# Top-k threshold search in a two-layer kernel: a third row counted on ScalarE, the test for equals moved to VectorE, GpSimd's sums beside the search cut into four pieces

## The chip, the cores and the metric

The kernel runs on one core of a Trainium2 chip. The metric is the device time of one execution in microseconds (us); the time of a kernel is the median of its runs.

## The reference

Two layers on 1024 tokens (T) of width 1024, in fp32. The change is in the first one, `hybrid_layer`, whose mixing half projects the normalised input once (`h @ w_in`) and gives part of the columns to a sparse attention and the rest to an RWKV7 scan:

```python
def dsa_attention(...):
    score = jnp.einsum('bth,bths->bts', wi, relu(jnp.einsum('bthd,bsd->bhts'...)))
    score = jnp.where(causal[None], score, -jnp.inf)
    _, sel = lax.top_k(score, 256)          # the 256 best keys of each query
    ...                                     # attention over the selected keys only
def rwkv7_group(p, mu_shift, w0, w_decay_up, a0, w_aaa_up, w_gate_up, ...):
    p = p + mu_shift * (p_prev - p)         # p_prev: the token before
    r, k, v, wd, ad, gd = jnp.split(p, splits, axis=-1)
    w_log = -softplus(-(w0 + tanh(wd) @ w_decay_up)) - 0.5
    a = sigmoid(a0 + ad @ w_aaa_up)
    g = sigmoid(gd) @ w_gate_up
    ...                                     # the scan, a group norm, times g
```

The output projection, an FFN and a second block (convolution, chunked attention, FFN, a gated per-layer embedding) follow; the change leaves them alone.

## The kernel before, in words

The framework's tile scheduler fixes the order of every engine's instructions when the kernel is built, from its own model of durations; on the chip each engine (PE = TensorE, DVE = VectorE, ACT = ScalarE, POOL = GpSimd, SP = SyncE, which issues loads and stores) works through its list in order and waits on semaphores where a tile that it reads or overwrites is not ready. Changing the cost or the number of a few instructions may therefore change the order of others, far from them.

Every fp32 product is made of three matmuls on a high and a low part (`mm3`, L105 to L107). A weight block of 128 columns is loaded (`load_cols`), its high part copied by ScalarE (L88) and its low part computed by GpSimd (L89), both in `split_w`, and `fm` then issues 48 matmuls of 512 columns.

The stage of the change is opened at L1875 and holds two streams that share no data.

The **projections of RWKV** (`Rwkv.proj`, TensorE). Fourteen blocks of `w_in`; each result in PSUM (three buffers of 128x1024) goes through `shift`: ScalarE writes it scaled (L1019) and a second time scaled and moved by one token (L1021), GpSimd adds the two (L1022), SP stores it. After every three blocks come the small products of one quarter of the decay, a and gate columns (`wl`, `gl`): weights split by L1064 and L1065, two evictions with a sigmoid (L1072) and one of the gate (L1080). There are four such quarters, so four gate evictions.

The **threshold search** (`Dsa.topk`, VectorE). Query blocks 2 to 7 give six rows j = 0 to 5 of 128 queries by 128 * (j + 3) scores. The 256th largest score of each query is found bit by bit: 15 rounds on the upper 16 bits, one count, 16 rounds on the lower 16 bits, 32 rounds in all. A round counts the scores at or above a candidate in each row: rows j < A on ScalarE, by Sign with an accumulator (L855, after `nv`, L850), the rest on VectorE (L846). Then VectorE compares the counts with K (L865), updates f (L866) and makes the next candidate (L863). No round starts before the counts of the one before are in, from both engines.

After the search each of the six rows is made into a mask: L909 marks and counts the scores above the threshold, L911 says how many of the equal ones are needed, L912 (GpSimd) marks the equal ones, L913 numbers them, L914 and L915 combine, and ScalarE writes the mask (L916). The buffers of this stage then become those of the next, attention (`attend`, its first product is L940) beside the chunked scan of RWKV, whose loads SP issues (L1111 to L1115, kHL at L962, qT at L963).

Of the kernel before, what the change touches and what calls it, by code (L numbers as in the profile page):

```python
# [8 lines left out]
FP = mybir.dt.float32  # L9
# [6 lines left out]
ALU = mybir.AluOpType  # L16
AX = mybir.AxisListType
PSUM = bass.MemoryType.PSUM
T = 1024
# [5 lines left out]
class Core:  # L25
# [56 lines left out]
        self.nc.sync.dma_start(raw, w[k * 128:(k + 1) * 128, :])  # L82
        return raw

    def split_w(self, raw):
        shp = list(raw.shape)
        hl = self.wp.tile([shp[0], 2] + shp[1:], FR, name="whl", tag="whl", bufs=self.nhl)
        self.nc.scalar.activation(hl[:, 0], raw, AF.Copy)  # L88
        self.nc.gpsimd.tensor_sub(hl[:, 1], raw, hl[:, 0].bitcast(FP))  # L89
        return hl  # L90

    def after(self):
# [102 lines left out]
def fm(c, w, kt, act, m0=0, m=128):  # L195

    return fms(c, [w], kt, act, m0, m)[0]


def fms(c, ws, kt, act, m0=0, m=128):  # L200

    act = Feat(act) if isinstance(act, list) else act
    ps = [c.psum([m, T]) for _ in ws]
    for hf in range(2):
        sl = slice(hf * 512, hf * 512 + 512)
        for p, w in zip(ps, ws):
            c.mm3(p[:, sl], [((w[:, 0, k, m0:m0 + m], w[:, 1, k, m0:m0 + m]), (act.cols(k, 0, hf), act.cols(k, 1, hf))) for k in range(kt)])
    return ps
# [433 lines left out]
class Dsa:  # L642
# [187 lines left out]
    def topk(self, ap):  # L830

        c, nc = self.c, self.nc
        N, A = 6, 2
        st, sti, tk1 = self.tk
        cnt, K, sg, vs, gtc, need, pos, k1, f, cand, nv = (st[:, j] for j in range(11))
        pre, low = sti[:, 0], sti[:, 1]
# [43 lines left out]
        for j in range(N):  # L880
            x = self.sc[j + 2]
# [12 lines left out]
        for j in range(N):  # L894
            if j < A:
                nc.vector.tensor_scalar(K[:, j:j + 1], K[:, j:j + 1], -128.0 * (j + 3), None, op0=ALU.add)
            nc.vector.scalar_tensor_tensor(h[j].bitcast(U16), h[j], f[:, j:j + 1], self.sc[j + 2].bitcast(U16)[:, 0::2],
                                           op0=ALU.is_equal, op1=ALU.mult)
# [5 lines left out]
        for j in range(N):  # L904
            n = (j + 3) * 128
            x = self.sc[j + 2]
            gt = ap.tile([128, n], BF, name="gt", tag="junk", bufs=1)
            eq = ap.tile([128, n], BF, name="eq", bufs=2)
            nc.vector.scalar_tensor_tensor(gt, x, sg[:, j:j + 1], vs[:, j:j + 1].to_broadcast([128, n]), op0=ALU.mult, op1=ALU.is_gt,  # L909
                                           accum_out=gtc[:, j:j + 1])  # L910
            nc.vector.tensor_scalar(need[:, j:j + 1], gtc[:, j:j + 1], -1.0, 256.0, op0=ALU.mult, op1=ALU.add)  # L911
            nc.gpsimd.tensor_scalar(eq, x, pre.bitcast(FP)[:, j:j + 1], None, op0=ALU.is_equal)  # L912
            nc.vector.tensor_tensor_scan(x, one.to_broadcast([128, n]), eq, 0.0, op0=ALU.mult, op1=ALU.add)  # L913
            nc.vector.scalar_tensor_tensor(x, x, need[:, j:j + 1], eq, op0=ALU.is_le, op1=ALU.mult)  # L914
            nc.vector.scalar_tensor_tensor(x, x, -1.0, gt, op0=ALU.add, op1=ALU.add)  # L915
            nc.scalar.activation(self.mk[j + 2], x, AF.Copy, scale=-NEG)  # L916
# [63 lines left out]
class Rwkv:  # L980
# [35 lines left out]
    def shift(self, ap, ps, j, out, m=128):  # L1016

        nc = self.nc
        nc.scalar.activation(out, ps, AF.Copy, scale=self.mu1[:m, j:j + 1])  # L1019
        t = ap.tile([m, T], FP, name="sh", tag="xo", bufs=4)  # L1020
        nc.scalar.activation(t[:, 1:], ps[:, :T - 1], AF.Copy, scale=self.mu[:m, j:j + 1])  # L1021
        nc.gpsimd.tensor_add(out[:, 1:], out[:, 1:], t[:, 1:])  # L1022

    def proj(self, hT, gd32, ap, beside):
        c, nc, p = self.c, self.nc, self.p
        w = p["w_in"]
        t4 = lambda n: ap.tile([128, T], FP, name=n, tag="xo", bufs=4)
        lo = lambda n, m=128: ap.tile([m, 2, T], FR, name=n, tag="lo", bufs=2)
        cols = lambda j: fm(c, c.split_w(c.load_cols(w, 456 + j * 128, 128, 8)), 8, hT)

        def rkv(pr):
            for q in range(3):
# [6 lines left out]
        x = t4("xl")  # L1039
# [4 lines left out]
        x = t4("xl")  # L1044
# [4 lines left out]
        x = t4("xl")  # L1049
# [5 lines left out]
        for pr in range(4):  # L1055
            m = slice(pr * 128, pr * 128 + 128)
            raw = ap.tile([128, 3, 128], FP, name="wl_raw", bufs=1)
# [8 lines left out]
            for rows, b, dst in ((slice(0, 64), self.w0, self.sgd), (slice(64, 128), self.a0, self.ad)):  # L1066
                ps = c.psum([128, T])
                for hf in range(2):
                    s = slice(hf * 512, hf * 512 + 512)
                    c.mm3(ps[:, s], [((wt[rows, 0, 0], wt[rows, 1, 0]), (wl[rows, 0, s], wl[rows, 1, s]))])  # L1070
                x = t4("xo")
# [3 lines left out]
            for hf in range(2):  # L1075
                s = slice(hf * 512, hf * 512 + 512)
                c.mm3(ps[:, s], [((wt[:, 0, 1], wt[:, 1, 1]), (gl[:, 0, s], gl[:, 1, s])),
                                 ((wt[0:32, 0, 2], wt[0:32, 1, 2]), (gl2[:, 0, s], gl2[:, 1, s]))])
            x = t4("xo")
# [1033 lines left out]
```

## Time and profile before

| | us |
|---|---|
| median of three runs | 3777.41 (3772.05 to 3777.46) |
| the profiled execution | 3769.52 |
| its span in the profile | 3767.8 |
| TensorE / VectorE / ScalarE / GpSimd busy in the span | 3326.7 / 1980.7 / 1298.1 / 1127.8 |
| the stage of the change, first projection column to last mask | 276.6 to 550.6 |
| attention beside the scan, the next stage | 566 to 1164 |

The span is the time from the first to the last instruction of the profiled execution; its own time has 1.7 us around that. TensorE is busy 88% of the span, the other engines much less, but these are averages over stages with different limits: the stage of the change is 7% of the span, and what limits it is read from its own rows. [...]

### The profile page before, as it was taken

The page shows a single profiled execution, that of the slowest core. Times are in us where ns is not written, and L with a number is a line of the kernel's source. Part 1 is how long each engine was busy: PE and PEld are TensorE (multiplying, and loading weights), DVE is VectorE, ACT ScalarE, POOL GpSimd, SP SyncE. Part 2 cuts the span into 40 slices and gives each one's busy share as a digit, 9 for nine tenths or more (in the row PEclk, how much of TensorE's full clock was granted, in tenths as well). Part 3 has the DMA queues.
Part 4 walks back from the last instruction along what each step waited for, and adds up shares of the span by engine and source line. Part 5 has one row for each costly group of instructions (what it writes and reads, how often), then busy time and mean ns, then how long its engine had stood idle before and what let it go on. Part 6 is the DMA issues. An engine that isn't in the chain of part 4 may idle for free. (4 is left out here: it accounts for less than half of the span.)

```text
span 3767.8 us, 42121 instructions
## 1 busy us (share of the span) xinstructions
PE 3326.7 (88%) x16048; PEld 2689.4 (71%) x16048; DVE 1980.7 (53%) x3181; ACT 1298.1 (34%) x2177; POOL 1127.8 (30%) x1007
## 2 busy tenths in 40 slices
PE   3788767898996899999998999989978899998988
PEld 2666545676774688888887788778856788876767
DVE  5569987667643412221225210026733688879983
ACT  3354433333333321111113211246633444444332
POOL 3214245434325322222223222131143222223441
PEclk7888865566567999999999999999989999998989
DMA  4552232212124321111113122210043322213244
GB/s 168 154 165 90 75 108 89 76 35 71 31 72 144 118 60 47 51 45 51 51 45 112 53 70 84 102 56 10 19 141 127 95 84 82 81 56 140 93 149 149
DMA packets 252218, 324.67 MB, mean 86 GB/s; under 512 B 16383, under 2 KB 193504, under 8 KB 250992
## 3 DMA queue, kind: packets, MB, share of 16 engines
q1 hardware_dynamic: 250960, 321.75, 26.9%
q8 instruction: 126, 2.06, 0.2%
q14 instruction: 76, 0.62, 0.1%
q0 software_dynamic: 1056, 0.23, 0.0%
HBM read 241.63 MB, written 80.29 MB: 85 GB/s over the span
## 5 line engine op out<-in xcount | busy, mean ns | idle before, releaser
L89 POOL TENSOR_TENSOR whl<-wraw,whl 128x1024 fp32r<-128x1024 f32 (+1 forms) x128 | 286.6, 2244 | 882.5 <-ACT whl L88 879.2
L105 PE MATMUL ps<-h,whl 128*128 128x512 f32 x1216 | 477.8, 395 | 17.7 <-ACT h L214 13.6
L106 PE MATMUL ps<-h,whl 128*128 128x512 f32 x1216 | 478.5, 394 | 3.5 <-POOL h L215 3.5
L107 PE MATMUL ps<-h,whl 128*128 128x512 f32 x1216 | 477.1, 392 | 0.0
L105 PEld LDWEIGHTS ps<-h,whl 128*128 128x128 f32 x1216 | 230.9, 190 | 69.3 <-ACT h L214 15.9
L88 ACT ACTIVATE whl<-wraw 128x1024 fp32r<-128x1024 f32 (+1 forms) x128 | 125.2, 988 | 440.8 <-issue 225.0
L106 PEld LDWEIGHTS ps<-h,whl 128*128 128x128 f32 x1216 | 231.1, 190 | 54.4 <-POOL h L215 6.4
L107 PEld LDWEIGHTS ps<-h,whl 128*128 128x128 f32 x1216 | 231.0, 190 | 48.4
L532 DVE TENSOR_TENSOR silu<-silu,ps 128x1024 f32<-128x1024 f32 x22 | 26.9, 1221 | 431.8 <-PE ps L107 431.8
L288 PE MATMUL ps<-h,op 128*128 128x512 f32 x616 | 237.4, 391 | 6.1 <-ACT op L311 5.2
L289 PE MATMUL ps<-h,op 128*128 128x512 f32 x616 | 240.4, 390 | 0.0
L290 PE MATMUL ps<-h,op 128*128 128x512 f32 x616 | 239.9, 390 | 0.0
L597 PE MATMUL o<-pT,v 128*128 128x256 f32 (+1 forms) x640 | 156.7, 364 | 13.7 <-ACT pT L592 7.7
L313 POOL TENSOR_TENSOR op<-t,op 128x512 fp32r<-128x512 f32 x44 | 73.3, 1666 | 305.1 <-ACT op L311 268.9
L592 ACT ACTIVATE pT<-tp 128x512 fp32r<-128x512 f32 (+2 forms) x221 | 94.6, 444 | 186.7 <-PE tp L589 149.9
L1388 DVE SCALAR_TENSOR_TENSOR cv<-up,v_fw,cv 128x1023 f32<-128x1023 f32 x88 | 134.1, 1524 | 30.0 <-ACT cv L1386 29.8
L105 PE MATMUL ps<-wo,h 128*128 128x512 f32 x320 | 128.9, 412 | 18.9 <-ACT wo L1398 16.5
L288 PE MATMUL ps<-op,op 128*128 128x512 f32 x308 | 123.9, 405 | 24.1 <-ACT op L412 14.9
L106 PE MATMUL ps<-wo,h 128*128 128x512 f32 x320 | 129.8, 411 | 15.1 <-POOL wo L1399 15.1
L597 PEld LDWEIGHTS o<-pT,v 128*128 128x128 f32 x640 | 116.8, 238 | 36.4 <-ACT pT L592 14.0
L846 DVE TENSOR_SCALAR_CACHE_REDUCE junk<-h,tk 128x640 bf16<-128x640 int16 (+7 forms) x128 | 137.9, 1077 | 3.4
L288 PEld LDWEIGHTS ps<-h,op 128*128 128x128 f32 x616 | 116.2, 189 | 30.9 <-ACT op L311 5.6
(593 smaller groups left out, 8118.1 us busy)
## 6 DMA issues: line engine op xcount, KB each, us to landing
wraw<-in_w_ffn_up_dram SPq DMA_DIRECT2D x66, 512.0 KB, 3.9
adaw<-in_ada_w_dram SPq DMA_DIRECT2D x96, 256.0 KB, 3.4
wraw<-in_w_in_dram SPq DMA_DIRECT2D x42, 512.0 KB, 4.0
wraw<-in_w_ffn_gate_dram SPq DMA_DIRECT2D x22, 512.0 KB, 3.9
wraw<-in_w_ffn_down_dram SPq DMA_DIRECT2D x22, 512.0 KB, 3.6
f_d<-cv SPq DMA_DIRECT2D x22, 512.0 KB, 2.6
raw<-in_w_ffn_down_dram SPq DMA_DIRECT2D x22, 512.0 KB, 7.7
raw<-f_d SPq DMA_DIRECT2D x22, 512.0 KB, 5.5
```

The lines of the kernel that those rows point to most:

```text
L88: self.nc.scalar.activation(hl[:, 0], raw, AF.Copy)
L89: self.nc.gpsimd.tensor_sub(hl[:, 1], raw, hl[:, 0].bitcast(FP))
L105: self.nc.tensor.matmul(out, lh, rh, start=first and i == 0, stop=False)
L106: self.nc.tensor.matmul(out, lh, rl, start=False, stop=False)
L107: self.nc.tensor.matmul(out, ll, rh, start=False, stop=last and i == n - 1)
L288: mm(out, lh, rh, start=start and i == 0, stop=False, skip_group_check=True)
L289: mm(out, lh, rl, start=False, stop=False, skip_group_check=True)
L290: mm(out, ll, rh, start=False, stop=stop and i == n - 1, skip_group_check=True)
L592: nc.scalar.activation(pT[:, 0, 0:n, q], x, AF.Copy)
L597: nc.tensor.matmul(o[:, q], v[:, b0 + s].rearrange("p a d -> p (a d)"), pT[:, x, s, q], start=b0 == 0 and n == 0, stop=end and n == 3)
L846: nc.vector.tensor_scalar(junk, x, thr, None, op0=ALU.is_ge, op1=ALU.add, accum_out=out)
L1388: nc.vector.scalar_tensor_tensor(out[:, s:], ps[:, :T - s], w[2 - s][:, j:j + 1], out[:, s:], op0=ALU.mult, op1=ALU.add)
```

## The change

Four edits. `split_w` can subtract in pieces, and the blocks of `w_in` in `Rwkv.proj` use four (128x256 each). The addition in `shift` is cut into four pieces (255 columns and three of 256). `A` goes from 2 to 3: ScalarE counts the row of 640 scores too, which also moves that row's copy to 16 bits (L885 for L887) to ScalarE and adds one to the two fix-ups of K (L879, L896). And the test for equals is issued on VectorE.

```diff
--- before.py
+++ after.py
@@ -82,11 +82,13 @@
         self.nc.sync.dma_start(raw, w[k * 128:(k + 1) * 128, :])
         return raw
 
-    def split_w(self, raw):
+    def split_w(self, raw, parts=1):
         shp = list(raw.shape)
         hl = self.wp.tile([shp[0], 2] + shp[1:], FR, name="whl", tag="whl", bufs=self.nhl)
         self.nc.scalar.activation(hl[:, 0], raw, AF.Copy)
-        self.nc.gpsimd.tensor_sub(hl[:, 1], raw, hl[:, 0].bitcast(FP))
+        n = shp[1] // parts
+        for a in range(0, n * parts, n):
+            self.nc.gpsimd.tensor_sub(hl[:, 1, a:a + n], raw[:, a:a + n], hl[:, 0, a:a + n].bitcast(FP))
         return hl
 
     def after(self):
@@ -830,7 +832,7 @@
     def topk(self, ap):
 
         c, nc = self.c, self.nc
-        N, A = 6, 2
+        N, A = 6, 3
         st, sti, tk1 = self.tk
         cnt, K, sg, vs, gtc, need, pos, k1, f, cand, nv = (st[:, j] for j in range(11))
         pre, low = sti[:, 0], sti[:, 1]
@@ -909,7 +911,7 @@
             nc.vector.scalar_tensor_tensor(gt, x, sg[:, j:j + 1], vs[:, j:j + 1].to_broadcast([128, n]), op0=ALU.mult, op1=ALU.is_gt,
                                            accum_out=gtc[:, j:j + 1])
             nc.vector.tensor_scalar(need[:, j:j + 1], gtc[:, j:j + 1], -1.0, 256.0, op0=ALU.mult, op1=ALU.add)
-            nc.gpsimd.tensor_scalar(eq, x, pre.bitcast(FP)[:, j:j + 1], None, op0=ALU.is_equal)
+            nc.vector.tensor_scalar(eq, x, pre.bitcast(FP)[:, j:j + 1], None, op0=ALU.is_equal)
             nc.vector.tensor_tensor_scan(x, one.to_broadcast([128, n]), eq, 0.0, op0=ALU.mult, op1=ALU.add)
             nc.vector.scalar_tensor_tensor(x, x, need[:, j:j + 1], eq, op0=ALU.is_le, op1=ALU.mult)
             nc.vector.scalar_tensor_tensor(x, x, -1.0, gt, op0=ALU.add, op1=ALU.add)
@@ -1019,14 +1021,16 @@
         nc.scalar.activation(out, ps, AF.Copy, scale=self.mu1[:m, j:j + 1])
         t = ap.tile([m, T], FP, name="sh", tag="xo", bufs=4)
         nc.scalar.activation(t[:, 1:], ps[:, :T - 1], AF.Copy, scale=self.mu[:m, j:j + 1])
-        nc.gpsimd.tensor_add(out[:, 1:], out[:, 1:], t[:, 1:])
+        for a in range(0, T, 256):
+            s = slice(max(a, 1), a + 256)
+            nc.gpsimd.tensor_add(out[:, s], out[:, s], t[:, s])
 
     def proj(self, hT, gd32, ap, beside):
         c, nc, p = self.c, self.nc, self.p
         w = p["w_in"]
         t4 = lambda n: ap.tile([128, T], FP, name=n, tag="xo", bufs=4)
         lo = lambda n, m=128: ap.tile([m, 2, T], FR, name=n, tag="lo", bufs=2)
-        cols = lambda j: fm(c, c.split_w(c.load_cols(w, 456 + j * 128, 128, 8)), 8, hT)
+        cols = lambda j: fm(c, c.split_w(c.load_cols(w, 456 + j * 128, 128, 8), 4), 8, hT)
 
         def rkv(pr):
             for q in range(3):
```

After the change lines from L89 on stand 2 lower, and lines behind `shift` 4 lower: L846 is L848, L855 is L857, L865 and L866 are L867 and L868, L909 is L911, L916 is L918, L1019 and L1021 are L1021 and L1023, L1022 is L1026, L1080 is L1084. VectorE loses 32 counts and a copy and gains six tests and two small operations; ScalarE gains 32 Signs and a copy; GpSimd has 29 whole sums (15 in `shift`, 14 in `split_w`) replaced by 116 pieces and loses the six tests; TensorE's matmuls are the same. The orders of TensorE, VectorE, ScalarE, GpSimd and SP differ through this stage and the next, and agree after that.

ScalarE at the end of the search, before: the last round's two Signs, then the masks of the six rows with the last evictions between them.

```order
L1019 ACTIVATE xo<-ps,mu_453 128x1024
L1021 ACTIVATE sh<-ps,v_c 128x1023
L855 ACTIVATE junka,tk<-h_3008,tk 128x384
L855 ACTIVATE junka,tk<-h_3008,tk 128x512
L916 ACTIVATE mk<-scb 128x384
L1019 ACTIVATE xo<-ps,mu_453 128x1024
L1021 ACTIVATE sh<-ps,v_c 128x1023
L1072 ACTIVATE xo<-ps,v_c 128x1024
L916 ACTIVATE mk<-scb 128x512
L1072 ACTIVATE xo<-ps,v_c 128x1024
L722 ACTIVATE nbt<-ps 128x383
L1080 ACTIVATE xo<-ps 128x1024
```

And the end of the same list now:

```order
L857 ACTIVATE junka,tk<-h_3095,tk 128x384
L857 ACTIVATE junka,tk<-h_3095,tk 128x512
L857 ACTIVATE junka,tk<-h_3095,tk 128x640
L1021 ACTIVATE xo<-ps,mu_453 128x1024
L1023 ACTIVATE sh<-ps,v_c 128x1023
L857 ACTIVATE junka,tk<-h_3095,tk 128x384
L1076 ACTIVATE xo<-ps,v_c 128x1024 x2
L857 ACTIVATE junka,tk<-h_3095,tk 128x512
L1084 ACTIVATE xo<-ps 128x1024
L857 ACTIVATE junka,tk<-h_3095,tk 128x640
L724 ACTIVATE nbt<-ps 128x383 x3
L918 ACTIVATE mk<-scb 128x384
```

The last gate eviction (L1080, now L1084) stood behind the whole search and two masks; it now stands between the second and the third Sign of the last round. Counted in these lists, 9, 17, 26 and 32 rounds had been begun ahead of the four gate evictions before, all Signs of the last one included, and 8, 16, 24 and 32 now, with the 640 row of the 32nd still to come.

ScalarE around the second gate eviction, now:

```order
L1021 ACTIVATE xo<-ps,mu_453 128x1024
L1023 ACTIVATE sh<-ps,v_c 128x1023
L88 ACTIVATE whl<-wraw 128x1024
L1076 ACTIVATE xo<-ps,v_c 128x1024
L857 ACTIVATE junka,tk<-h_3095,tk 128x384
L1076 ACTIVATE xo<-ps,v_c 128x1024
L857 ACTIVATE junka,tk<-h_3095,tk 128x512
L1084 ACTIVATE xo<-ps 128x1024
L1068 ACTIVATE wl_hl<-wl_raw 128x256
L1068 ACTIVATE wl_hl<-wl_raw 32x128
L857 ACTIVATE junka,tk<-h_3095,tk 128x640
L857 ACTIVATE junka,tk<-h_3095,tk 128x384
L857 ACTIVATE junka,tk<-h_3095,tk 128x512
```

The two sigmoid evictions (L1076) and the gate eviction stand between the Signs of one round. Before, the round's two Signs stood behind both sigmoid evictions, with the gate eviction and the split of the next quarter's weights between them:

```order
L1019 ACTIVATE xo<-ps,mu_453 128x1024
L1021 ACTIVATE sh<-ps,v_c 128x1023
L88 ACTIVATE whl<-wraw 128x1024
L1072 ACTIVATE xo<-ps,v_c 128x1024 x2
L855 ACTIVATE junka,tk<-h_3008,tk 128x384
L1080 ACTIVATE xo<-ps 128x1024
L1064 ACTIVATE wl_hl<-wl_raw 128x256
L1064 ACTIVATE wl_hl<-wl_raw 32x128
L855 ACTIVATE junka,tk<-h_3008,tk 128x512
L855 ACTIVATE junka,tk<-h_3008,tk 128x384
```

VectorE behind the search, before, the first two of six rows:

```order
L909 SCALAR_TENSOR_TENSOR gt,tk<-scb,tk 128x384
L911 TENSOR_SCALAR tk<-tk 128x1
L913 SCALAR_TENSOR_TENSOR scb<-tk_483,eq 128x384
L914 SCALAR_TENSOR_TENSOR scb<-scb,tk,eq 128x384
L915 SCALAR_TENSOR_TENSOR scb<-scb,gt 128x384
L909 SCALAR_TENSOR_TENSOR gt,tk<-scb,tk 128x512
L911 TENSOR_SCALAR tk<-tk 128x1
L913 SCALAR_TENSOR_TENSOR scb<-tk_483,eq 128x512
L914 SCALAR_TENSOR_TENSOR scb<-scb,tk,eq 128x512
L915 SCALAR_TENSOR_TENSOR scb<-scb,gt 128x512
```

And now:

```order
L905 TENSOR_TENSOR tk<-tki,tk 128x6
L914 TENSOR_SCALAR eq<-scb,tki 128x384
L914 TENSOR_SCALAR eq<-scb,tki 128x512
L911 SCALAR_TENSOR_TENSOR gt,tk<-scb,tk 128x384
L913 TENSOR_SCALAR tk<-tk 128x1
L915 SCALAR_TENSOR_TENSOR scb<-tk_483,eq 128x384
L916 SCALAR_TENSOR_TENSOR scb<-scb,tk,eq 128x384
L917 SCALAR_TENSOR_TENSOR scb<-scb,gt 128x384
L914 TENSOR_SCALAR eq<-scb,tki 128x640
L911 SCALAR_TENSOR_TENSOR gt,tk<-scb,tk 128x512
```

The test for equals (L914) of a row stands one or two rows ahead of its use, among the operations that mark, number and combine.

## Rows read from the trace of the kernel before

**Rows 1.** Windows between gate evictions: us, busy by engine, TensorE clock, DMA, GB/s.

```profile
276.60:363.50 86.90, 69.08 (x269) 53.08 (x269) 72.70 (x131) 42.97 (x68) 41.00 (x26) 0.85 0.31 95
363.50:419.00 55.50, 48.23 (x177) 36.50 (x177) 53.27 (x104) 23.55 (x47) 15.97 (x8) 0.81 0.30 98
419.00:477.90 58.90, 40.62 (x160) 30.32 (x159) 55.83 (x111) 25.97 (x52) 15.23 (x8) 0.82 0.25 83
477.90:531.10 53.20, 46.28 (x172) 34.97 (x172) 50.47 (x101) 21.91 (x42) 20.07 (x11) 0.82 0.14 56
sum 254.50, PE 204.22 PEld 154.87 DVE 232.26 ACT 114.40 POOL 92.27; mean PE 51.06 PEld 38.72 DVE 58.07 ACT 28.60 POOL 23.07
```

**Rows 2.** Timeline of VectorE, an undisturbed round: start us, us, instruction.

```profile
333.61 0.87 DVE L846 TENSOR_SCALAR_CACHE_REDUCE junk<-h,tk 128x640 bf16<-128x640 int16 x1
...
334.52 1.01 DVE L846 TENSOR_SCALAR_CACHE_REDUCE junk<-h,tk 128x768 bf16<-128x768 int16 x1
...
338.85 0.87 DVE L846 TENSOR_SCALAR_CACHE_REDUCE junk<-h,tk 128x640 bf16<-128x640 int16 x1
```

**Rows 3.** Timeline of ScalarE in the same round.

```profile
333.80 0.62 ACT L855 ACTIVATE junka<-h,tk 128x384 bf16<-128x384 int16 x1 [3.70 <-DVE tk L850]
...
334.54 0.72 ACT L855 ACTIVATE junka<-h,tk 128x512 bf16<-128x512 int16 x1
```

**Rows 4.** Timeline of VectorE at the end of a disturbed round.

```profile
381.40 1.74 DVE L865 TENSOR_TENSOR tk<-tk 128x6 f32<-128x6 f32 x1
383.18 2.33 DVE L866 SCALAR_TENSOR_TENSOR tk<-tk 128x6 f32<-128x6 f32 x1
```

**Rows 5.** Timeline of GpSimd at the same place.

```profile
380.73 2.39 POOL L1022 TENSOR_TENSOR xo<-xo,sh 128x1023 f32<-128x1023 f32 x1 [14.70 <-issue]
383.08 2.40 POOL L89 TENSOR_TENSOR whl<-wraw,whl 128x1024 fp32r<-128x1024 f32 x1
```

**Rows 6.** Groups by line, 307 to 516: busy, mean ns | idle before, releasers.

```profile
L866 DVE SCALAR_TENSOR_TENSOR tk<-tk 128x6 f32<-128x6 f32 x30 | 22.1, 737 | 1.4 <-DVE tk L865 0.5
L865 DVE TENSOR_TENSOR tk<-tk 128x6 f32<-128x6 f32 x31 | 18.1, 584 | 3.3
L1021 ACT ACTIVATE sh<-ps,v_c 128x1023 f32<-128x1023 f32 x12 | 13.2, 1101 | 0.0
...
L105 PE MATMUL ps<-gl,wl_hl 128*128 128x512 f32 (+1 forms) x12 | 9.5, 792 | 36.1 <-ACT sh L1021 36.1
```

**Rows 7.** Timeline of VectorE in the six rows after the search.

```profile
516.84 0.86 DVE L909 SCALAR_TENSOR_TENSOR gt<-scb,tk 128x384 bf16<-128x384 f32 x1
...
527.49 2.80 DVE L914 SCALAR_TENSOR_TENSOR scb<-scb,tk,eq 128x640 f32<-128x640 f32 x1
...
543.14 1.28 DVE L909 SCALAR_TENSOR_TENSOR gt<-scb,tk 128x1024 bf16<-128x1024 f32 x1
```

**Rows 8.** Groups by line on VectorE, 516 to 551.

```profile
L909 DVE SCALAR_TENSOR_TENSOR gt<-scb,tk 128x384 bf16<-128x384 f32 (+5 forms) x6 | 8.3, 1375 | 0.2
```

**Rows 9.** Line L882: min/median/max ns, first and last start, forms.

```profile
L882 DVE TENSOR_SCALAR scb<-scb,tk x6: 420/582/749, 302.3 to 304.7; 128x384 f32<-128x384 f32 x1, 128x512 f32<-128x512 f32 x1, 128x640 f32<-128x640 f32 x1, 128x768 f32<-128x768 f32 x1
```

**Rows 10.** Timeline of ScalarE, the last mask.

```profile
549.53 1.06 ACT L916 ACTIVATE mk<-scb 128x1024 bf16<-128x1024 f32 x1 [5.00 <-DVE scb L915]
```

**Rows 11.** Timeline of SP's queue behind the last mask.

```profile
550.61 0.37 SPq L1111 DMA_DIRECT2D sg<-sg_d  x1
...
554.86 0.59 SPq L963 DMA_DIRECT2D qT<-q_d  x1
```

**Rows 12.** Timeline of TensorE, start of the next stage.

```profile
566.28 0.44 PE L940 MATMUL qk<-kHL,qT 128*128 128x128 f32 x1 [17.50 <-DMA qT<-q_d]
```

**Rows 13.** Timeline of GpSimd, tests of the first rows and a 128x256 sum.

```profile
516.71 5.41 POOL L912 TENSOR_SCALAR eq<-scb,tki 128x384 bf16<-128x384 f32 x3 [5.97 <-DVE tki L902]
...
570.79 0.66 POOL L933 TENSOR_TENSOR nb<-near,mk 128x256 f32<-128x256 f32 x1
```

**Rows 14.** Window of the next stage, columns as in rows 1.

```profile
566.00:1164.00 598.00, 524.72 (x3497) 406.37 (x3497) 390.30 (x1021) 208.88 (x467) 237.60 (x360) 0.61 0.20 59
```

## The prediction

> **What bounds the kernel now.** I read the stage of the change first, by windows cut where ScalarE starts a gate eviction (the end of a group of projection columns) [rows 1]. [...] Then one round of the search on each engine: VectorE needs 338.85 - 333.61 = 5.24 us with nothing in its way [rows 2], and ScalarE sits idle 3.70 us before its two Signs [rows 3]. So the rounds are VectorE's. Third, what lengthens them: small VectorE operations that take 0.17 us alone took 1.74 and 2.33 [rows 4] while GpSimd ran whole sums of 2.4 us [rows 5]; both end when GpSimd's do. Over the stretch L866 and L865 cost 22.1 + 18.1 us for 61 instructions [rows 6], 61 x 0.17 = 10.4 of it their own, so 29.8 us are waiting, 0.96 per round.
>
> TensorE, the other stream, is held by the same rounds: its wl/gl products sat idle 36.1 us for evictions L1021 [rows 6], which stand on ScalarE behind Signs that wait for VectorE. The 58.9 us between the second and third gate evictions are nine rounds of 5.24 + 0.96 = 55.8 and little else, while TensorE had 40.6 us of work there [rows 1].
>
> Last, what waits for the search's end: the six rows start at 516.84 [rows 7], the last mask is written at 549.53 + 1.06 [rows 10], SP's first load follows at 550.61 and qT's at 554.86 [rows 11], and TensorE, idle 17.50 us, begins the next stage at 566.28 behind qT [rows 12]. A microsecond saved before the last mask is therefore a microsecond of the kernel, unless the next stage loses it.
>
> **The change part by part.**
> (a) *Third row to ScalarE.* VectorE loses the 640 count, 334.52 - 333.61 = 0.91 us per round [rows 2]: 5.24 - 0.91 = 4.33, 29.1 us over 32 rounds. ScalarE's two Signs start 0.74 apart and last 0.62 and 0.72 [rows 3]; 0.10 more per 128 columns makes the third 0.82, an estimate, with steps of 0.74, 0.84, 0.94: 2.5 us a round. It begins 0.27 after VectorE's state is set and is done within 2.8 of 4.33 us. The copies and fix-ups (one copy moved to ScalarE, two tiny VectorE operations) are under 1 us once; nothing.
> (b) *GpSimd's sums in four pieces.* A 128x256 sum took 0.66 us [rows 13], so four take 2.6 for 2.4 and GpSimd (41.0 us busy in the first window, 15 to 20 in the others [rows 1]) has room. A small operation should wait for one piece rather than a whole sum, at best 0.33 on average instead of 1.2. Bounds of the saving: nothing (GpSimd starts the next piece before VectorE gets in) to 29.8 us (no waits left). I take half, 15 us, on VectorE's side.
> (c) *Which stream then sets the end.* In the new order each gate eviction stands behind exactly eight rounds' first Signs, and the last round's third Sign stands behind the last gate eviction; before, all 32 rounds were done ahead of that eviction. Eight rounds take 8 x 4.33 = 34.6 us, with all of the old waits 8 x 5.29 = 42.3. TensorE's busy time in the last three windows is (48.23 + 40.62 + 46.28) / 3 = 45.0 per group [rows 1]. So the order of the two is reversed: TensorE, not the search, paces the groups, and the end follows TensorE's work plus its idle time: first column 276.60 + 204.2 busy + idle + the gate eviction (about 1.1, as L1021's mean [rows 6]) + Sign 0.94 + five small steps of 0.2. That is 483.8 + idle for the start of the six rows, against 516.84: a shift of idle - 33.0.
> The idle time before was 254.5 - 204.2 = 50.3. Its causes were the rounds. What stays is ScalarE's in-order queue at the turn of a group: the pair L1019/L1021 (1.1 us each [rows 6]) before a PSUM buffer is free, and up to two Signs (1.8) ahead of it: 4 per group, 16 in all. Ends: 0 and 41.6 (50.3 shrunk only as the rounds are, x 4.33 / 5.24). I take 16, since the rounds no longer fill a group: shift -17.0.
> (d) *Test for equals on VectorE.* Beside GpSimd's tests (three of them 5.41 us together [rows 13]), L909 took 8.3 us for six shapes [rows 8], where 1.28 for 1024 columns [rows 7], when GpSimd's last test was over, scales to 1.28 x 4224 / 1024 = 5.3: 3.0 saved. L914's 2.80 for 640 columns [rows 7] was mostly a wait for GpSimd's sum; scaled from 1.28 it is 0.80, and with one piece of waiting some 1.1: 1.7 saved. The six tests now cost VectorE 6 x 0.58 = 3.5, by the single-source operation of the same shapes, L882 [rows 9]; by 1.28 per 1024 columns 5.3. Together -1.2, between -5 and +1.
> [...]
> (e) *After the masks.* SP issues kHL first and the other loads behind it; qT stays 4.25 us behind the first load to within 1. The orders of the next stage differ in many places; I price them at nothing, with 10 us to either side (1.7% of its 598 us [rows 14]).
>
> Sum: -17.0 - 1.2 = **-18.2 us**. The profiled execution took 3769.52 us, 7.9 below the median of the runs, 3777.41, so 3751.3 by its measure and **3759** by the median's.
>
> **The rivals.** A measurement of this kernel tells about 0.2%, 7.6 us, from no change. By the sum the result is idle - 34.2; it leaves "the same" under an idle time of 26.6 and turns slower above 41.8.
> *B, VectorE's floor.* If TensorE keeps the full clock, with gaps gone (204.2 us at a mean of 0.83 would shrink), its busy time falls and the search paces again at its new speed: 29.1 us less, up to 15 more by the pieces, 1.2 by (d): -30 to -45, about 3740. For it: TensorE's gaps are what rows 1 show beside the low clock. Against: the wl/gl products stay split between evictions.
> *C, ScalarE's queue locks the two streams together (slower).* Three Signs instead of two stand before each eviction, and evictions that wait for TensorE now stand before Signs on which VectorE waits; in particular the last round waits for the last gate eviction. If TensorE's idle time stays at 41.6 to 50.3, the six rows start at 525 to 534 instead of 516.84: +7 to +16, about 3789; with 27 to 41 it is a draw. For it: the 36.1 us on L1021. Against: those waits come of rounds that are then 1 to 2 us shorter and fewer per group.
> *D, the next stage gives it back.* Attention and scan share all engines from 566 to 1164 with TensorE busy 524.7 of 598 us [rows 14]; a worse interleaving by 3% (18 us) would leave 3777.
> *E, the pieces do nothing.* GpSimd keeps its turn between pieces and the waits stay 0.96 a round. Then eight rounds are 42.3, still under 45.0: the forecast stands within some 5 us, and B is cut to -30.
>
> **How the numbers follow.** The forecast (idle 8 to 25, E in it) 0.55; B 0.20; C 0.15, of it 0.08 a draw and 0.07 slower; D 0.10, of it 0.06 a draw, 0.02 slower and 0.02 still faster. Faster: 0.55 + 0.20 + 0.02 = 0.77; same 0.14; slower 0.09. The range must hold the forecast with the 10 us of (e), most of B and the draws: 3735 to 3778.
>
> **What would show it.** Right: three counts per round on VectorE (L848), a free round near 4.33 us; small operations with no duration above some 0.9; the wait of wl/gl products for L1023 well under 36 us; six rows from about 500; last mask near 532; the next stage as long as before. Wrong: free rounds near 5 us with VectorE idle for a Sign (ScalarE the bound); small operations still at 2.3 (E); the last gate eviction at or after 520 with TensorE idle ahead of it (C); first product of the next stage 15 us or more earlier but no gain at its end (D).

## The result, and the profile after

The change takes 3749.42 us (median of 15 runs, 3733.43 to 3766.28) against 3775.8 us of the kernel before (15 runs beside it, 3764.22 to 3781.5): a ratio of 0.9932, 95% interval 0.9915 to 0.995, or 26 us faster. The forecast was 18 us faster, 3759, with a range of 3735 to 3778. The profiled execution took 3752.12 us, with a span of 3750.4.

The windows between gate evictions, the change (columns as in rows 1):

```profile
276.60:354.90 78.30, 69.02 (x282) 53.35 (x282) 57.96 (x108) 48.47 (x81) 47.60 (x62) 0.91 0.37 113
354.90:402.90 48.00, 42.73 (x169) 32.83 (x169) 39.15 (x85) 31.46 (x62) 18.72 (x25) 0.89 0.30 98
402.90:451.00 48.10, 42.85 (x169) 32.98 (x170) 39.82 (x87) 31.67 (x63) 20.35 (x28) 0.89 0.32 106
451.00:499.05 48.05, 43.99 (x169) 34.21 (x169) 35.45 (x80) 29.44 (x61) 12.32 (x18) 0.86 0.16 66
sum 222.45, PE 198.59 PEld 153.38 DVE 172.37 ACT 141.04 POOL 98.99; mean PE 49.65 PEld 38.34 DVE 43.09 ACT 35.26 POOL 24.75
```

Against [rows 1] the groups are 48 us apart instead of 53 to 59, the last gate eviction comes at 499.05 instead of 531.06, and it is VectorE that has room now, 172.4 us busy of 222.5 (232.3 of 254.5 before). TensorE is busy 198.6 us and idle 23.9; 50.3 before. The windows start at 276.60, as before; in this execution the first projection column starts at 278.26, so that 1.7 us of the first window are still work of the stage ahead.

The timeline of VectorE at the end of the search, the change:

```profile
487.83 1.01 DVE L848 TENSOR_SCALAR_CACHE_REDUCE junk<-h,tk 128x768 bf16<-128x768 uint16 x1
...
492.14 1.00 DVE L848 TENSOR_SCALAR_CACHE_REDUCE junk<-h,tk 128x768 bf16<-128x768 uint16 x1
...
495.58 0.08 DVE L848 DVE_READ_ACCUMULATOR junk<-h,tk 128x1 f32 x1
500.91 0.17 DVE L867 TENSOR_TENSOR tk<-tk 128x6 f32<-128x6 f32 x1 [5.25 <-ACT junka L857]
...
501.80 0.81 DVE L914 TENSOR_SCALAR eq<-scb,tki 128x384 bf16<-128x384 f32 x2
```

A free round is 492.14 - 487.83 = 4.31 us, 5.24 before [rows 2]. Behind it stands the new wait: VectorE's own counts of the last round are in at 495.58 + 0.08 = 495.66, but L867 starts 5.25 us later, behind a Sign. The timeline of ScalarE shows why:

```profile
488.01 0.61 ACT L857 ACTIVATE junka<-h,tk 128x384 bf16<-128x384 uint16 x1 [1.81 <-DVE tk L852]
...
488.75 0.72 ACT L857 ACTIVATE junka<-h,tk 128x512 bf16<-128x512 uint16 x1
...
489.60 0.83 ACT L857 ACTIVATE junka<-h,tk 128x640 bf16<-128x640 uint16 x1
...
499.05 1.02 ACT L1084 ACTIVATE xo<-ps 128x1024 f32<-128x1024 f32 x1 [3.22 <-PE ps L109]
499.97 0.82 ACT L857 ACTIVATE junka<-h,tk 128x640 bf16<-128x640 uint16 x1
...
532.67 1.06 ACT L918 ACTIVATE mk<-scb 128x1024 bf16<-128x1024 f32 x1 [5.34 <-DVE scb L917]
```

Three Signs of a free round start 0.74 and 0.85 apart and the third lasts 0.83 [rows 3 for the first two]. The last round's third Sign, at 499.97, stands behind the gate eviction, which itself waited 3.22 us for TensorE. The last mask follows at 532.67; it was at 549.53 [rows 10]. The forecast had asked for three counts, 4.33 us, six rows from about 500 and the mask near 532.

Groups by line over the search, the change, answering [rows 6]:

```profile
L107 PE MATMUL ps<-gl,wl_hl 128*128 128x512 f32 (+1 forms) x16 | 12.7, 793 | 19.4 <-ACT sh L1023 19.4
...
L868 DVE SCALAR_TENSOR_TENSOR tk<-tk 128x6 f32<-128x6 f32 x30 | 9.9, 330 | 1.0
L865 DVE TENSOR_SCALAR tk<-tk 128x6 f32<-128x6 f32 x30 | 9.6, 319 | 1.0
L867 DVE TENSOR_TENSOR tk<-tk 128x6 f32<-128x6 f32 x30 | 9.3, 309 | 28.8 <-ACT junka L857 26.6
...
L852 DVE TENSOR_SCALAR tk<-tk 128x6 f32<-128x6 f32 x31 | 8.2, 265 | 1.0
...
L899 DVE SCALAR_TENSOR_TENSOR h<-h,tk,scb 128x768 uint16<-128x768 int16 (+5 forms) x6 | 7.3, 1264 | 0.0
```

The four small operations of a round wait for GpSimd 9.9 + 9.6 + 9.3 + 8.2 - 121 x 0.17 = 16.4 us in all, half of what they did before (29.8 in two of them alone). But VectorE is idle 26.6 us in nine waits for Signs, of which it had none before, and with the last round's 5.25 that makes 31.9. This all but closes the account of the search: from VectorE's first count, 308.7, to the six rows, 501.8, are 193.1 us. Of these 32 x 4.31 = 137.9 are rounds, 16.4 waits for GpSimd and 31.9 waits for Signs; 6.9 are left, and the change from upper to lower bits (L899) takes 7.3.

kHL's loads on SP's queue before, which stand between the lines of [rows 11], and qT's load, with its us from issue to landing at the end:

```profile
553.54 1.27 SPq L962 DMA_DIRECT2D kHL<-k_d  x2
...
qT<-q_d SPq DMA_DIRECT2D x1, 512.0 KB, 11.3
```

The same now, with TensorE's first product of the next stage:

```profile
516.66 1.27 SPq L964 DMA_DIRECT2D kHL<-k_d  x2
533.75 0.38 SPq L1115 DMA_DIRECT2D sg<-sg_d  x1
...
536.22 0.47 SPq L965 DMA_DIRECT2D qT<-q_d  x1
...
542.80 0.44 PE L942 MATMUL qk<-kHL,qT 128*128 128x128 f32 x1 [26.83 <-DMA near<-nbz]
...
qT<-q_d SPq DMA_DIRECT2D x1, 512.0 KB, 6.4
```

kHL's loads, behind the last mask before, are now issued 16 us ahead of it, at 516.66, and qT follows the first load behind the mask by 2.5 us in place of 4.25. It also lands 6.4 us after its issue in place of 11.3, when kHL's loads stood just ahead of it. From the end of the last mask (533.73) to the first product are 9.1 us; before it was 15.7 [rows 10, 12].

### The profile page after: what moved, and what is told of

Its sections match the earlier page's. It is cut to its first block, busy times and chain, and to the rows that moved or that the text cites. A ratio compares the mean times of both kernels' runs of the same rounds, so it can differ in the third digit from the quotient of the medians.

```text
span 3750.4 us, 42196 instructions
## 1 busy us (share of the span) xinstructions
PE 3320.9 (89%) x16048; PEld 2688.3 (72%) x16048; DVE 1934.5 (52%) x3124; ACT 1327.4 (35%) x2242; POOL 1129.8 (30%) x1088
## 5 line engine op out<-in xcount | busy, mean ns | idle before, releaser
L91 POOL TENSOR_TENSOR whl<-wraw,whl 128x1024 fp32r<-128x1024 f32 (+2 forms) x170 | 294.3, 1746 | 885.3 <-ACT whl L88 844.8
L107 PE MATMUL ps<-h,whl 128*128 128x512 f32 x1216 | 478.0, 395 | 17.6 <-ACT h L216 13.5
L107 PEld LDWEIGHTS ps<-h,whl 128*128 128x128 f32 x1216 | 231.1, 191 | 69.3 <-ACT h L216 15.9
L599 PE MATMUL o<-pT,v 128*128 128x256 f32 (+1 forms) x640 | 154.0, 358 | 19.4 <-ACT pT L594 10.9
L1392 DVE SCALAR_TENSOR_TENSOR cv<-up,v_fw,cv 128x1023 f32<-128x1023 f32 x88 | 134.1, 1524 | 30.0 <-ACT cv L1390 29.8
L290 PE MATMUL ps<-op,op 128*128 128x512 f32 x308 | 123.4, 404 | 24.4 <-ACT op L414 14.5
L107 PE MATMUL ps<-wo,h 128*128 128x512 f32 x320 | 128.7, 412 | 17.8 <-ACT wo L1402 14.6
L107 PE MATMUL ps<-whl,fT 128*128 128x512 f32 x352 | 137.5, 391 | 0.3
```

Source lines behind the costliest of these rows:

```text
L91: self.nc.gpsimd.tensor_sub(hl[:, 1, a:a + n], raw[:, a:a + n], hl[:, 0, a:a + n].bitcast(FP))
L107: self.nc.tensor.matmul(out, lh, rh, start=first and i == 0, stop=False)
L290: mm(out, lh, rh, start=start and i == 0, stop=False, skip_group_check=True)
L599: nc.tensor.matmul(o[:, q], v[:, b0 + s].rearrange("p a d -> p (a d)"), pT[:, x, s, q], start=b0 == 0 and n == 0, stop=end and n == 3)
L1392: nc.vector.scalar_tensor_tensor(out[:, s:], ps[:, :T - s], w[2 - s][:, j:j + 1], out[:, s:], op0=ALU.mult, op1=ALU.add)
```

## The experiments

Twelve experiments; each was compared with the kernel before on the same chip. Times in the profile of each are of one execution: where TensorE's first projection column starts, where the six rows after the search begin (their first operation), where the last mask starts, and the first attention product. The medians are of 4 runs, of 10 for e2 and e10 and of 15 for the change. e8 and e9, which leave work out, and e12 ran once: 3765.83, 3716.47 and 3764.53 us.

| kernel | first column | six rows | last mask | first product | median, us | ratio to before, 95% interval |
|---|---|---|---|---|---|---|
| before | 276.6 | 516.7 | 549.5 | 566.3 | 3775.8 | |
| the change | 278.3 | 501.8 | 532.7 | 542.8 | 3749.4 | 0.9932 (0.9915 to 0.995) |
| e1 third row | 276.1 | 497.4 | 530.4 | 540.1 | 3742.3 | 0.9909 (0.9893 to 0.9924) |
| e2 cut sums | 273.9 | 504.9 | 537.1 | 551.0 | 3778.5 | 1.0011 (0.9998 to 1.0024) |
| e3 equals | 275.8 | 515.1 | 547.5 | 557.3 | 3760.0 | 0.9953 (0.9937 to 0.9969) |
| e5 third row, cut sums | 274.5 | 498.9 | 530.4 | 541.4 | 3740.8 | 0.9913 (0.9886 to 0.994) |
| e6 third row, equals | 276.8 | 498.2 | 530.9 | 540.3 | 3732.6 | 0.9897 (0.988 to 0.9914) |
| e4 change, products spread | 276.7 | 488.9 | 519.7 | 529.9 | 3734.2 | 0.9885 (0.9863 to 0.9907) |
| e7 products spread, third row | 277.1 | 493.2 | 524.7 | 534.4 | 3735.1 | 0.9893 (0.9869 to 0.9917) |
| e11 the same with equals | 278.7 | 494.9 | 527.0 | 537.0 | 3729.8 | 0.9882 (0.9865 to 0.9899) |
| e10 change, four rows | 276.6 | 521.3 | 551.5 | 561.6 | 3786.5 | 1.003 (1.0011 to 1.005) |

The executions reach the first column up to 5 us apart, two of the same program (e12) 3.4, so what a kernel gains in the stage is counted below from its first column.

**The parts alone (e1 to e3).** Each keeps one edit of the change and undoes the others:

```diff
e1:  -        N, A = 6, 2
     +        N, A = 6, 3
e2:  -        self.nc.gpsimd.tensor_sub(hl[:, 1], raw, hl[:, 0].bitcast(FP))
     +        for a in range(0, n * parts, n):
     ...
e3:  -            nc.gpsimd.tensor_scalar(eq, x, pre...
     +            nc.vector.tensor_scalar(eq, x, pre...
```

e1: 

> Only the third row is moved to ScalarE; GpSimd's sums are whole again and the test for equals is GpSimd's. My theory (the rounds paced both streams, and with shorter rounds TensorE paces the groups): a free round is 4.33 us, small operations still wait up to 2.3, some 0.9 a round, so eight rounds are about 42, just under TensorE's 43 to 45 per group. Gate evictions 48 to 52 us apart, six rows from about 503 to 510 (501.8 in the change, 516.8 before), last mask 536 to 544: -8 to -15 us before the next stage, half or more of the change's gain. Rival 1 (the pieces made the gain): the rounds stay as long as their waits, six rows at 513 or later, no gain over 4 us. Rival 2 (the gain is the next stage's new order): the last mask moves by less than 5 us and the total still falls by 15.

e2: 

> Only GpSimd's sums are cut in four. My theory: the free round stays 5.24 us, the waits of small operations halve (0.96 to about 0.5 a round, 15 us over the search), the search still paces, VectorE stays busy over 90%: six rows at 502 to 509, total -7 to -13 us. Rival 1 (the pieces made the gain): six rows at 502 or earlier and -17 or more. Rival 3 (GpSimd keeps its turn between pieces): waits as before, 516, nothing gained.

e3: 

> Only the test for equals is moved to VectorE. My theory: the search is as before (six rows near 516), the six rows shorten by some 3 us (L909's 8.3 us to 5.2, L914's wait gone, tests 3.5 added, against 33.8 before): last mask 546 to 550, total -1 to -4 us, a draw. [...]

At the last mask, counted from the first column, the third row alone gives 19 us, as much as the whole change; the cut sums alone 10, the test alone 1. So Rival 1 falls. My theories hold only in part. The third row alone gives more than I expected of e1 (8 to 15 us; six rows from 503, mask from 536). In e3 the six rows shorten by 0.4 us, not by 3 (33.9 before from their start to the end of the last mask, 33.5), and its total is 16 us lower, not 1 to 4. VectorE's small operations with the cut sums alone, over the search:

```profile
L852 DVE TENSOR_SCALAR tk<-tk 128x6 f32<-128x6 f32 x31 | 12.4, 400 | 1.0
...
L868 DVE SCALAR_TENSOR_TENSOR tk<-tk 128x6 f32<-128x6 f32 x31 | 10.3, 332 | 1.5 <-DVE tk L867 0.5
L865 DVE TENSOR_SCALAR tk<-tk 128x6 f32<-128x6 f32 x30 | 9.8, 328 | 1.0
L867 DVE TENSOR_TENSOR tk<-tk 128x6 f32<-128x6 f32 x31 | 8.3, 268 | 4.9 <-ACT junka L857 1.8
```

They wait 12.4 + 10.3 + 9.8 + 8.3 - 123 x 0.17, about 20 us. Before, the other two of the four, beside those of [rows 6], were:

```profile
L863 DVE TENSOR_SCALAR tk<-tk 128x6 f32<-128x6 f32 x30 | 7.3, 242 | 1.0
...
L850 DVE TENSOR_SCALAR tk<-tk 128x6 f32<-128x6 f32 x31 | 5.3, 170 | 1.0
```

So all four waited 22.1 + 18.1 + 7.3 + 5.3 - 122 x 0.17, about 32 us: 12 more, near the 10 gained at the last mask. With the third row alone the same lines:

```profile
L867 DVE TENSOR_TENSOR tk<-tk 128x6 f32<-128x6 f32 x31 | 17.6, 567 | 27.8 <-ACT junka L857 25.7
L868 DVE SCALAR_TENSOR_TENSOR tk<-tk 128x6 f32<-128x6 f32 x31 | 11.6, 373 | 1.1
...
L852 DVE TENSOR_SCALAR tk<-tk 128x6 f32<-128x6 f32 x31 | 5.5, 178 | 1.0
L865 DVE TENSOR_SCALAR tk<-tk 128x6 f32<-128x6 f32 x30 | 5.3, 178 | 1.0
```

Here the sums are whole, and yet the waits are 40.0 - 123 x 0.17, about 19 us: 10 small operations lasted over 1 us, before it was 16. That shorter rounds and the waits at Signs keep them out of a sum's way fits this, but is not shown. Cutting the sums then saves 3 us more (16.4 in the change), not 12.

The totals do not follow the masks. e2 is 10 us early at the last mask and 13 at the first product, but no faster in ten runs; e3 is 8 early at the first product and 16 faster. That is the next stage's doing, below.

**The change without one part (e5, e6).** e5 is the change with the test on GpSimd, e6 the change with whole sums:

```diff
e5:  -            nc.vector.tensor_scalar(eq, x, pre...
     +            nc.gpsimd.tensor_scalar(eq, x, pre...
e6:  -        cols = ... c.load_cols(w, 456 + j * 128, 128, 8), 4), 8, hT)
     +        cols = ... c.load_cols(w, 456 + j * 128, 128, 8), 1), 8, hT)
     -        for a in range(0, T, 256):
     +        for a in range(0, T, T):
```

e5: 

> The change without the test for equals on VectorE. My theory after the single parts: with the third row moved TensorE paces the groups, so cutting the sums, though it halves the waits of small operations, has nothing to give any more: six rows at 495 to 503, as with the third row alone (497.5) or the change (501.8), last mask 528 to 536. Rival (the parts add up: third row -19 and pieces -12 at the last mask): six rows at 488 or earlier.

e6: 

> The change without the cut sums. My theory: six rows at 495 to 503, and the six rows' stretch 30 to 32 us (33.0 with the third row alone, whose test is GpSimd's): last mask 526 to 534. Rival (the pieces carry the gain): six rows at 508 or later.

Last masks at 530.4 and 530.9: all four kernels with a third row stand within 2.5 us, counted from the first column within 2, with or without cut sums and with either engine for the test. The parts do not add up, as expected; in the search stage the third row is the whole gain of the change. From the start of e6's six rows to that of its last mask are 32.7 us where 30 to 32 were expected, 33.0 in e1: there too the test saves 0.4. In the totals the change has the highest ratio of the four, and e6's interval lies just below the change's, so no total shows a gain from cutting the sums.

**Who holds whom (e8, e9).** e8 leaves TensorE 16 matmuls of 48 in each of the 14 blocks, e9 half of the rounds:

```diff
e8:  -  cols = lambda j: fm(c, c.split_w(...), 8, hT)
     +  ... for hf in range(2):
     +          for k in range(8):
     +              nc.tensor.matmul(ps[...], wt[:, k % 2, k], hT[k][:, 0, ...], start=k == 0, stop=k == 7)
e9:  -            for b in range(bits - 1, -1, -1):
     +            for b in range(bits - 1, bits // 2 - 1, -1):
```

e8: 

> The change with one product of three in the 14 blocks of projection columns, 16 matmuls in place of 48 (the other two are left out, so r, k, v are inexact). My theory (TensorE's work paces the groups after the change): with it gone the search runs at its own speed, 32 rounds of 4.33 + 0.5 us: six rows at 470 to 482 (501.8 in the change), VectorE's wait for the third Sign behind a gate eviction nearly gone. Rival (ScalarE's order of evictions and Signs holds the search, whatever TensorE has to do): six rows at 495 or later.

e9: 

> The change with half of the search's rounds: each of the two searches stops after its upper bits, 17 counting rounds in place of 32, so other keys are selected. This is the mirror of the light products, which left the six rows at 500.6 with a third of TensorE's work. Theory 1 (TensorE's own work paces the groups): the gate evictions hardly move, the last at 485 to 497 (499.0 in the change), 44 to 48 us apart. Theory 2 (the rounds, through ScalarE's queue, pace TensorE): the last gate eviction at 470 or earlier, groups under 42 us. Theory 3 (neither alone: the two streams hold each other at ScalarE, and each alone would be near 480): last gate eviction 475 to 487, TensorE's idle time in the stage falls from 23.9 to 5 to 12 us.

e8's search, on VectorE's timeline and in the waits from 307 to 500:

```profile
499.90 0.81 DVE L914 TENSOR_SCALAR eq<-scb,tki 128x384 bf16<-128x384 f32 x2
...
DVE tk L867 <- ACT junka L857: 25.4, 7, 5.4
```

The six rows begin at 499.90, 1.9 us before the change's: with a third of TensorE's work in the blocks my theory asked for 470 to 482, and it is wrong. The order has moved too: the evictions are bunched, the last gate eviction comes at 438.8, the 19 rounds up to 441 take 7.0 us each and the last 13 take 4.5. VectorE still waits 25.4 us for Signs. e9's gate evictions, ScalarE's timeline:

```profile
349.67 1.02 ACT L1084 ACTIVATE xo<-ps 128x1024 f32<-128x1024 f32 x1 [2.27 <-PE ps L109]
...
399.03 1.02 ACT L1084 ACTIVATE xo<-ps 128x1024 f32<-128x1024 f32 x1 [2.28 <-PE ps L109]
...
445.22 1.02 ACT L1084 ACTIVATE xo<-ps 128x1024 f32<-128x1024 f32 x1
...
484.78 1.02 ACT L1084 ACTIVATE xo<-ps 128x1024 f32<-128x1024 f32 x1 [1.82 <-PE ps L109]
```

While the search ran two of them were 49.4 us apart; the group in which it ended, at 411, took 46.2, and the last, with no Signs on ScalarE, 39.6. So TensorE's stream alone is faster than 48 us a group as well, and Theory 3 gives the last eviction (484.8), though not the idle time: to 480 TensorE is busy 183.5 of 203.4 us. So by these two neither stream alone sets the pace. What fits both kernels is that they hold each other where they meet, in ScalarE's queue. In the change itself both waits are in the trace: TensorE's for L1023 (19.4 us in the groups by line above) and VectorE's for Signs (31.9). But the two orders differ from the change's, so for the change this is an inference; e4 and e10 bear on it.

**Room at ScalarE (e4, e7, e11).** The small products of a quarter stood behind every third block of columns; here each stands behind a block of its own:

```diff
-        rkv(0)
         for pr in range(4):
...
             for q, (rows, b, dst) in enumerate(...):
+                col(pr, q)
                 ps = c.psum([128, T])
...
+            col(pr, 2)
             ps = c.psum([128, T])
...
-            if pr < 3:
-                rkv(pr + 1)
```

`col(pr, q)` is one pass of the loop of `rkv`. e7 has e4's order with the edit of e6 and that of e5, e11 with the edit of e6 alone.

e4: 

> The change, with the three small products of a quarter spread: one behind each block of projection columns, in place of all three behind every third block. My theory: TensorE's idle time left (23.9 us, 22.2 of it the gate products waiting for L1023) comes of three PSUM buffers in a row being taken with no long work between; spread, each eviction has a block's 48 matmuls to hide behind. TensorE's idle time falls to 5 to 10, VectorE's wait for the third Sign (26.6 us) falls too, last gate eviction at 480 to 488 (499.0 in the change), total 10 to 18 us below the change. Rival (ScalarE's order, not PSUM, is what both wait for): idle time stays near 20 and the total stays with the change's.

e7: 

> The small products spread, the third row on ScalarE, sums whole, test for equals on GpSimd. Here TensorE no longer paces (last gate eviction 484.7 with the products spread, six rows 488), so by my theory the search's own speed counts again and whole sums cost: waits of 0.9 a round in place of 0.5, 13 us over the search: six rows at 493 to 503, total 3737 to 3752 (3734 with the cut sums). Rival (cut sums are of no use even then): six rows at 485 to 491, total as with them or below.

e11: 

> The small products spread, third row on ScalarE, test for equals on VectorE, sums whole: the combination of the two versions that are lowest so far (products spread 3734, third row with equals 3733). The search stage by its parts: six rows at 491 to 495 as with the test on GpSimd (493.3), last mask 521 to 524. What the next stage does is not foreseen by any theory here: with the same 3516 matmuls it has taken 586 to 621 us from the first attention product, so the total may be 3710 to 3750.

e4's gate products, its stage as one window, and VectorE's waits for Signs:

```profile
L107 PE MATMUL ps<-gl,wl_hl 128*128 128x512 f32 (+1 forms) x16 | 7.6, 472 | 0.0
...
276.60:484.70 208.10, 188.04 (x774) 145.11 (x774) 167.98 (x352) 139.35 (x261) 96.74 (x129) 0.95 0.31 102
...
DVE tk L867 <- ACT junka L857: 21.2, 12, 2.9
```

The last gate eviction comes at 484.7 and the six rows at 488.9, 11 us before the change's if counted from the first column, with the same instructions. TensorE's idle time is 208.1 - 188.0 = 20.1, not the 5 to 10 expected, and that is the rival's sign, though the total is not: the gate products wait no more (19.4 us in the change), but others do. What fell is TensorE's busy time, by 9 us of the stage's own, at a granted clock of 0.95 of full speed in place of 0.86 to 0.91 (the gate products of L107 took 0.47 us on the mean, 0.79 in the change), and VectorE's waits for Signs, from 31.9 to 21.2. So e4 shows that the order of these products costs the change 11 us, but the reason I gave for it, TensorE's idle time, is not where most of it went. With whole sums (e7, e11) the six rows are 4 us later: here the search's own speed counts again, as expected, though less than 13. In the totals the three cannot be told apart; all lie below the change, e4's and e11's intervals clear of the change's.

**Four rows (e10).**

```diff
-        N, A = 6, 3
+        N, A = 6, 4
```

> The change with four rows on ScalarE (Sign of 768 columns too). VectorE's free round would be 4.33 - 1.06 = 3.27 us, ScalarE's four Signs 0.74 + 0.84 + 0.94 + 1.04 = 3.6 after a start of 0.27: the free round becomes 3.9 to 4.1, bound by ScalarE. If the evictions' time on ScalarE adds to the rounds: 16 x 3.3 us of evictions and copies that no longer fit in ScalarE's slack, six rows at 505 to 530, slower than the change. If TensorE alone paces: six rows at 497 to 504 still. If the rounds pace: 490 to 497.

VectorE's waits, ScalarE's last gate eviction and a free round on VectorE:

```profile
DVE tk L867 <- ACT junka L857: 89.3, 30, 8.8
...
478.48 1.02 ACT L1084 ACTIVATE xo<-ps 128x1024 f32<-128x1024 f32 x1 [0.48 <-PE ps L109]
...
507.66 1.14 DVE L848 TENSOR_SCALAR_CACHE_REDUCE junk<-h,tk 128x896 bf16<-128x896 uint16 x1
...
511.44 0.17 DVE L867 TENSOR_TENSOR tk<-tk 128x6 f32<-128x6 f32 x1 [1.31 <-ACT junka L857]
...
512.13 1.14 DVE L848 TENSOR_SCALAR_CACHE_REDUCE junk<-h,tk 128x896 bf16<-128x896 uint16 x1
```

VectorE waits for a Sign in 30 rounds, 89.3 us, and the kernel is slower than before. A free round takes 512.13 - 507.66 = 4.47 us, more than with three rows, and 1.31 of it is a wait for the last Sign, so some 40 us of the 89.3 are the Signs' own length. The other 50 come near the 16 x 3.3 = 53 us of evictions and copies expected: their time on ScalarE does add to the rounds, once its Signs set their length. TensorE is not held by it: its last gate eviction comes at 478.5, 20 us before the change's, since this order puts 6 rounds and not 8 ahead of each, and the last 8 of the 32 rounds run behind it.

**The same program again (e12),** with no edit.

> The change itself a second time, for the scatter of one program: its 15 runs spread over 33 us (3733 to 3766), its first profile was 3752 with the six rows at 501.8, last mask at 532.7, and 608.1 us from the first attention product to the first output-projection weight of the next stage. If that stage's 586 to 621 us over the kernels of this study are set by the order of instructions, it is again 604 to 612, and the search stage within 1 us; if they are chance of the execution (the granted clock), it may lie anywhere from 590 to 620 while the search stage stays within 1 us.

The next stage, from the first attention product to the first weight of the output projection, columns as in rows 1; the change's first profile:

```profile
542.80:1150.90 608.10, 530.31 (x3516) 411.83 (x3516) 396.42 (x1026) 211.79 (x472) 235.80 (x360) 0.62 0.21 60
```

and the same program's second:

```profile
540.20:1163.70 623.50, 547.79 (x3516) 426.56 (x3516) 396.35 (x1026) 211.94 (x472) 235.71 (x360) 0.59 0.20 58
```

The last mask came at 530.2 (532.7 the first time), the total was 3764.5. But the first column had started at 274.9, not 278.3: from there to the last mask are 255.3 us against 254.4, so the search stage repeats within 1 us, as expected. The next stage took 608.1 us once and 623.5 the other time, outside the range of either theory, with the same 3516 matmuls, TensorE busy 17 us longer at a lower granted clock, 0.59 in place of 0.62. After it the two differ by a constant again. So that stage is where executions of one program scatter, and one profile of it tells nothing on an order within some 15 us. Over the profiles of the table it lasted 586.5 (e6, clock 0.64) to 620.2 us (e10, 0.60). The medians say more. For the change the total (26 us) agrees with the first product (25.1 us early from the first column, and 24.4 in e12), so the next stage gives and takes nothing; for e2 it gives all 13 us back, for e6 and e11 it adds 13. What in those orders decides it, no run here shows.

## Why the prediction was right, by its own steps

- **(a) Third row.** Right: 4.31 us for a round where 4.33 was forecast, 0.83 for the Sign where 0.82 was.
- **(b) Cut sums.** The waits halved, as forecast, but 13 of the 16 us came with the third row alone (19 us of waits beside whole sums, not 30), and e1 and e5 have the same last mask. One small operation (L867 at 330.93) still took 1.75 us, over the 0.9 that was to be the longest: it met one of GpSimd's sums that the change leaves whole (L217, 2.37 us from 330.28), and the two end within 0.03 us of each other. Rival E, that the pieces do nothing, comes near it in the time, though not in the waits.
- **(c) The shift of the six rows.** Forecast -17.0, measured 501.80 - 516.84 = -15.0, and -16.7 from the first column. That is in part luck: from the first column TensorE was busy 196.9 us instead of 204.2 and idle 23.9 instead of 16, two errors that cancel. The idle time has the cause that the step named, the wait for L1023 at the turn of a group, but is 6 a group and not 4. The step that failed is that TensorE, not the search, paces the groups. e8 took most of its work away and the six rows stayed; e9's last group took 39.6 us, less than the 45 of busy time that the step had for TensorE's floor; and in e1 the six rows begin 6 us ahead of the last gate eviction (503.4), so the end does not hang on it. In its place stand waits in both directions at ScalarE: TensorE's for L1023, VectorE's for Signs. Rival C named that mechanism and priced it as a loss from 41 us of idle time on; with three Signs it is 23.9. The loss with four (e10) is another one, a search held by ScalarE alone: TensorE was idle only 14 us up to its last gate eviction.
- **(d) The six rows.** Forecast -1.2, measured 533.73 - 501.80 = 31.9 against 33.8: -1.8. The test's move gives some 0.5 of it (e1 to e6, e5 to the change), the cut sums 1.5 or more (e1 to e5, e6 to the change).
- **(e) After the masks.** Mis-sized: priced at nothing, it gave 6.6 us. "qT stays 4.25 us behind the first load" was 2.47, and qT's load took 6.4 us in place of 11.3. I read that kHL moved ahead of the other loads, but not that it would no longer wait for the last mask; its loads, issued from 516.66 and landing within 6.4 us, are done before qT's begins at 536.22. In e2, where they still stand behind the mask, the first product came 12.8 us after it; in the other kernels of the table that have an edit, where kHL is loaded ahead of the mask, 8.3 to 9.9.
- **The next stage**, priced at nothing with 10 us to either side, gave nothing on the median, but single executions differ by more, and in e2 it takes back 13 us over ten runs, as rival D has it, in another kernel than the one forecast.

Together, from the first column, -16.7 - 1.8 - 6.6 = -25.1 at the first product, which is the measured gain within its interval; the forecast was 7 us short because of (e).

## What to carry to other kernels

Work moved to an engine that also runs evictions in order is paid in waits: three rows cost 32 us of them and still gained, four cost 89 and lost, because the engine's own work then set the length of nearly every round. Try the parts of a change singly: two parts that shorten the same wait do not add up, and one of them may be free to leave out. And read a stage's gain from its start to its end, where it repeated within 1 us here, then the total by many runs: a later stage at a wavering clock (here 608.1 us at 0.62 and 623.5 at 0.59) can hide or lend 15 us.

## What the runs showed of the hardware that was not expected

In the change, single-source operations wait for GpSimd's pieces too: L865 and L852 took up to 0.67 and 0.66 us with a median of 0.17, near the length of a piece (0.74 in the median), where the forecast had charged two-input ones, L866 and L865 of [rows 6]. L865 at 332.91 ended at 333.58, and the piece of L91 that had begun at 332.82 ended at 333.55. Before, L863 did so once, 2.31 us beside a whole sum of 2.39, and was at 0.17 otherwise. The test for equals did it in e6, where one of six took 2.63 us beside a whole sum (2.36 us from 498.55) and the median was 0.65:

```profile
L914 DVE TENSOR_SCALAR eq<-scb,tki x6: 415/646/2632, 498.2 to 518.1; 128x384 bf16<-128x384 f32 x1, 128x512 bf16<-128x512 f32 x1, 128x640 bf16<-128x640 f32 x1, 128x768 bf16<-128x768 f32 x1
...
498.55 2.36 POOL L1026 TENSOR_TENSOR xo<-xo,sh 128x1023 f32<-128x1023 f32 x1 [9.68 <-issue]
```

TensorE's granted clock was 0.62 and 0.59 of full speed in the same stage of the same program. These are means: in stretches of half a microsecond of the change's first profile it was 0.50 in 175 and 1.00 in 11 of the 190 from 600 to 695 us, and in the stage of the change 0.50 in 33 and 1.00 in 153 of the 190 from 280 to 375. What differed ahead of it in the two executions the profiles do not tell.
